# Attention on one core: a planner's list of steps replaced by a finished order

## The chip, the cores and the metric

The kernel runs on one core of a Trainium2 chip. The metric is device time in microseconds of one launch; lower is better. TensorE (PE in the profile) does matmuls, ScalarE (ACT) and VectorE (DVE) elementwise work, GpSimd (POOL) the same and DMA issues, SyncE (SP) DMA issues alone. Each engine takes its instructions strictly in the order in which the program lists them.

## The reference

Grouped-query attention: 8 batches, 8 query heads, 2 key/value heads, 1024 positions, head size 64, all float32.

```python
for g in range(n_kv_heads):
    q_group = q[:, g*4:(g+1)*4]; k_group = k[:, g:g+1]; v_group = v[:, g:g+1]
    scores = np.matmul(q_group, k_group.transpose(0, 1, 3, 2)) / np.sqrt(64)
    attn = np.exp(scores - scores.max(-1, keepdims=True))
    output[:, g*4:(g+1)*4] = np.matmul(attn / (attn.sum(-1, keepdims=True) + 1e-08), v_group)
```

The kernel leaves the maximum out, which changes nothing at this size of scores, and divides after the second matmul.

## The kernel before, in words

There are 64 jobs, one for each batch and head, numbered b * 8 + h. A job is cut into 8 tiles along the keys. A tile is 128 keys by 1024 queries of scores: two concurrent matmuls of 64 rows (line 761, a "pair") write it to one of three slots of PSUM, `sp0` to `sp2`, of two banks each. A tile is then turned into exponentials in one of two ways.

- On ScalarE: one activation (line 771) from the slot to a bfloat16 tile `pt`. 368 of the 512 tiles go this way.
- On VectorE: 144 tiles. A first pass (line 783, `p` in the list below) scales the scores and writes 16-bit integers `yt`, which frees the slot. A chain of one or two such tiles then gets three steps out of SBUF: the mantissa part `zt` (line 792, "zh"), the exponent part `et` (line 800, "two"), and the product of `yt` and `zt` (line 810, "mul"). The exponential is the sum of `et` and `zt`; the output matmuls add it by reading both tiles, and in the last three jobs VectorE adds it itself (line 816). Columns of the product are given to GpSimd in pieces (line 739). VectorE and GpSimd do not use the shared port at the same time: a piece is tied to run beside the passes out of PSUM.

The output matmuls (line 829) take a 128 x 128 block of exponentials as weights and 65 columns of `va`, which are the 64 columns of v and a column of ones for the sum. Eight pieces of 128 queries make a job; seven pieces fill a bank (`ops`), then VectorE takes reciprocals of the sums (line 894) and multiplies (line 904) into `ost`, and SyncE stores a job of 256 KB (line 913). Jobs 0 and 63 are done tile by tile (lines 849 and 869).

Inputs come in by DMA. GpSimd's queue casts q, k and v from float32 to bfloat16 in DRAM (line 519; from job 4 on two jobs of q at a time). SyncE's queue transposes q (line 588) and k (line 578) into SBUF and copies the two halves of the transposed k to each other's partitions (lines 582 and 583), so that tiles 4 to 7 can be read as well, and loads v (line 571). A DMA on SyncE whose input has not landed holds up those behind it.

What sets the order: `Plan` walks through a string `ORDER` of steps and gives each step a model time from constants (the `M_` lines). The events are sorted by that time and emitted. `W` in the string means that PE's model waits; a score is only placed when its slot is free in the model. When casts, transposes and copies go out is worked out from the model time at which a job's first score is due (`need`): the transposes of q 11 us ahead of it, of k 12.5, the copies 6.5.

Of the kernel before, what the change touches and what calls it, by code (L numbers as in the profile page):

```python
# [108 lines left out]


class Chain:


    def __init__(self, id, nsteps):
        self.id, self.nsteps = id, nsteps
        self.pairs = []
# [4 lines left out]
        self.zend = INF
        self.end = 0

class State:
    pass


class Plan:

    def __init__(self, nj, npt, nct, nyt):
        self.nj, self.npt, self.nct, self.nyt = nj, npt, nct, nyt

# [3 lines left out]
        self.groups += [(i, min(i + PB, self.last)) for i in range(NPIECE, self.last, PB)]  # L140
# [807 lines left out]
```

## Time and profile before

| what | value |
| --- | --- |
| median of three runs | 353.0 us (352.84 to 353.11) |
| span of the profiled execution, first to last instruction | 350.8 us |
| own time of the profiled execution | not listed apart from its span; the median is 2.2 us above the span |
| PE busy (matmuls, ends modelled) | 342.2 us |
| ACT busy | 342.3 us |
| DVE busy | 340.5 us |
| POOL busy | 276.9 us |

Busy time is the union of an engine's instructions. Instructions that overlap in their pipelines make an engine look busy though the next one started late, so for ACT and DVE the distance between starts says more than the busy share. A row of the timeline is start, length, engine, line, operation, output<-input, shape and count of merged instructions; in brackets the idle time ahead of it and what ended it. A row of the groups is count, busy time, mean of one in ns, idle time ahead of them and what ended it. In a row by windows each engine's busy time is followed by the number of its instructions in brackets, then come the granted clock of PE, the share of the DMA engines and GB/s.

### The profile page before, as it was taken

The page shows a single profiled execution, that of the slowest core. Times are in us where ns is not written, and L with a number is a line of the kernel's source. Part 1 is how long each engine was busy: PE and PEld are TensorE (multiplying, and loading weights), DVE is VectorE, ACT ScalarE, POOL GpSimd, SP SyncE. Part 2 cuts the span into 40 slices and gives each one's busy share as a digit, 9 for nine tenths or more (in the row PEclk, how much of TensorE's full clock was granted, in tenths as well). Part 3 has the DMA queues.
Part 4 walks back from the last instruction along what each step waited for, and adds up shares of the span by engine and source line. Part 5 has one row for each costly group of instructions (what it writes and reads, how often), then busy time and mean ns, then how long its engine had stood idle before and what let it go on. Part 6 is the DMA issues. An engine that isn't in the chain of part 4 may idle for free.

```text
span 350.8 us, 14254 instructions
## 1 busy us (share of the span) xinstructions
PE 342.2 (98%) x6272; PEld 224.9 (64%) x6272; DVE 340.5 (97%) x517; ACT 342.3 (98%) x372; POOL 276.9 (79%) x265
## 2 busy tenths in 40 slices
PE   7899999999999999999999999999999999999995
PEld 3466666666666666666666666666666676666674
DVE  5999999999999999999999999999999999999995
ACT  6999999999999999999999999999999999999994
POOL 3268889799999999898999998999989958982000
PEclk9999999999999999999999999999999999999999
DMA  6899766496749757769896977297767994453223
GB/s 150 121 165 167 140 120 146 84 151 139 136 92 137 148 124 134 129 132 124 125 157 120 151 138 122 64 191 135 122 127 107 170 168 119 107 122 74 69 76 109
DMA packets 96574, 44.84 MB, mean 128 GB/s; under 512 B 61168, under 2 KB 95344, under 8 KB 95728
## 3 DMA queue, kind: packets, MB, share of 16 engines
q1 hardware_dynamic: 94128, 31.34, 43.8%
q0 software_dynamic: 2096, 12.19, 26.5%
q8 instruction: 49, 0.80, 1.1%
q10 hardware_dynamic: 288, 0.39, 0.3%
q14 instruction: 13, 0.11, 0.1%
HBM read 27.13 MB, written 28.97 MB: 160 GB/s over the span
## 4 chain that ended last, share of the span: by engine, by line
PE 60%; ACT 21%; DVE 15%; issue 1%; DMA 1%; DVEq 0%
PE ops L829 32%; PE sp L761 27%; ACT pt L771 21%; DVE yt L783 8%; DVE et L800 2%; DVE ost L904 2%; DVE zt L792 1%; DVE zt L810 1%; DMA q<-in_q_dram 1%; PE sp L869 1%; DVE rec L894 1%; PE sp L644 0%; DVE qt L662 0%; ACT q L633 0%; DVEq L943 0%
## 5 line engine op out<-in xcount | busy, mean ns | idle before, releaser
L771 ACT ACTIVATE pt<-sp 128x1024 bf16<-128x1024 f32 x368 | 339.8, 1036 | 0.5 <-PE sp L761 0.3
L739 POOL TENSOR_TENSOR zt<-yt,zt 128x560 bf16<-128x560 bf16 (+15 forms) x151 | 238.3, 1583 | 28.3 <-DVE zt L792 10.1
L829 PE MATMUL ops<-va,pt 128*128 128x65 bf16 x2840 | 177.0, 194 | 0.0
L783 DVE TENSOR_SCALAR yt<-sp 128x1024 uint16<-128x1024 f32 x144 | 174.9, 1215 | 1.3 <-PE sp L761 1.2
L761 PE MATMUL sp<-qt,kt 64*128 64x512 bf16 x1024 | 168.9, 382 | 3.2 <-ACT pt L771 1.7
L829 PEld LDWEIGHTS <-pt 128*128 128x128 bf16 x2840 | 131.5, 97 | 32.8 <-issue 32.8
L829 PE MATMUL ops<-va,zt 128*128 128x65 bf16 x1128 | 131.1, 194 | 0.0
L829 PE MATMUL ops<-va,et 128*128 128x65 bf16 x1096 | 125.3, 194 | 0.0
L829 PEld LDWEIGHTS <-et 128*128 128x128 bf16 x1096 | 87.9, 98 | 15.2 <-issue 15.0
L829 PEld LDWEIGHTS <-zt 128*128 128x128 bf16 x1128 | 91.2, 97 | 9.6 <-issue 9.2
L761 PEld LDWEIGHTS <-kt 64*128 64x128 bf16 x1024 | 50.9, 93 | 59.0 <-issue 36.0
L792 DVE TENSOR_SCALAR zt<-yt 128x2048 uint16<-128x2048 uint16 (+1 forms) x73 | 49.8, 683 | 0.5
L800 DVE TENSOR_SCALAR et<-yt 128x2048 uint16<-128x2048 uint16 (+1 forms) x73 | 49.0, 675 | 0.0
L904 DVE TENSOR_TENSOR ost<-ops,rec 128x448 f32<-128x448 f32 (+2 forms) x73 | 44.7, 612 | 0.5
L810 DVE TENSOR_TENSOR zt<-yt,zt 128x928 bf16<-128x928 bf16 (+17 forms) x64 | 39.1, 611 | 0.0
L519 POOL DMA_DIRECT2D qd<-in_q_dram x33 | 21.6, 655 | 4.4 <-PE sp L761 3.6
L894 DVE RECIPROCAL rec<-ops 128x7 f32<-128x7 f32 (+2 forms) x73 | 14.5, 199 | 0.1
L734 POOL MEMSET tick<- 128x1 bf16 x57 | 12.0, 211 | 0.0
L519 POOL DMA_DIRECT2D kd<-in_k_dram x8 | 5.3, 657 | 5.1 <-PE sp L761 5.1
L621 PE MATMUL ops<-warm 128*128 128x128 bf16 (+1 forms) x24 | 4.6, 334 | 1.2 <-DVE warm L513 1.2
L519 POOL DMA_DIRECT2D vd<-in_v_dram x8 | 5.6, 700 | 0.0
L621 PEld LDWEIGHTS <-warm 128*128 128x128 bf16 x24 | 2.0, 114 | 3.5 <-issue 2.3
(39 smaller groups left out, 27.4 us busy)
## 6 DMA issues: line engine op xcount, KB each, us to landing
out_dram<-ost SPq DMA_DIRECT2D x63, 256.0 KB, 3.1
qd<-in_q_dram POOLq DMA_DIRECT2D x29, 256.0 KB, 5.0
kt<-kt SPq DMA_DIRECT2D x30, 64.0 KB, 3.4
va<-vd SPq DMA_DIRECT2D x30, 64.0 KB, 3.1
kd<-in_k_dram POOLq DMA_DIRECT2D x7, 256.0 KB, 4.5
vd<-in_v_dram POOLq DMA_DIRECT2D x7, 256.0 KB, 5.3
qt<-qd SPq DMA_TRANSPOSE x63, 4.5
qd<-in_q_dram POOLq DMA_DIRECT2D x5, 128.0 KB, 4.0
```

Of the source, the lines that this page charges most:

```text
L519: return nc.gpsimd.dma_start(out=t.rearrange("(a x) d -> a (x d)", a=128), in_=src.rearrange("(a x) d -> a (x d)", a=128),)
L734: early = nc.gpsimd.memset(tick, 0.0)
L739: begun[j] = gps = nc.gpsimd.tensor_tensor(out=z, in0=flat(yt[j])[:, lo : lo + w], in1=z, op=ALU.mult)
L761: now = nc.tensor.matmul(sps[x][:, half, :], lhsT=t[lo : lo + D, c // NH, ci % NH * 128 : (ci % NH + 1) * 128], rhs=qt[j][lo : lo + D, 0, ...
L771: exps.append(nc.scalar.activation(out=p, in_=where_s[(j, c)], func=AF.Exp, scale=scale))
L783: vec = nc.vector.tensor_scalar(out=yt[ch][:, i, :, :], in0=where_s[c], scalar1=EXP_A, scalar2=EXP_B, op0=ALU.mult, op1=ALU.add,)
L792: vec = nc.vector.tensor_scalar(out=zt[j][:, 0:c], in0=yt[j][:, 0:c], scalar1=0x7F, scalar2=0x3F00, op0=ALU.bitwise_and, op1=ALU.bitwise_or,)
L800: vec = ins = nc.vector.tensor_scalar(out=et[j][:, 0:c], in0=yt[j][:, 0:c], scalar1=0x7F80, scalar2=None, op0=ALU.bitwise_and,)
L810: vec = nc.vector.tensor_tensor(out=z, in0=flat(yt[j])[:, 0 : cols[0]], in1=z, op=ALU.mult)
L829: ended[job] = nc.tensor.matmul(ops[plan.group_of[x] % 2][:, lo : lo + D + 1], lhsT=p[:, qs * 128 : (qs + 1) * 128], rhs=va[(b * G + h // ...
L894: vec = nc.vector.reciprocal(out=to, in_=sums)
L904: vec = nc.vector.tensor_tensor(out=to, in0=src, in1=by, op=ALU.mult)
```

## The change

The planner goes: the model constants, `State`, `Plan` and its sorting by time are removed. `ORDER` is now the finished list of instructions for all engines, in which every step stands as it is to be emitted, DMAs among them, with the slot that a score uses and the columns that GpSimd takes. New letters: `A0` a ScalarE score into slot 0, `a1` to `g1` a score for VectorE of the job 0 to 6 ahead into slot 1, `x` the activation, `p` VectorE's first pass, `z`, `t`, `m`, `+` the steps of the chain so many chains back, `G1,197` a piece of 8 x 197 columns of the chain one back, `V` three output matmuls, `r` and `n` reciprocal and normalisation, `S` a store, `X`, `q`, `Y`, `k`, `Z`, `v` casts, `T`, `K` transposes, `C` the two copies of k, `U` loads of v. `W` is gone: a score stands where it stands, and PE waits there if the slot is not free.

- A VectorE tile is now mostly three or four jobs ahead of ScalarE's (124 of 144 tiles); before, mostly one (82), at most two.
- `yt`, `et` and `zt`, pools of 6, 8 and 8 chains, become two rings of 22 tiles, `ye` and `zz`. The exponent step works in place on `ye`, so it now stands behind the product and waits for GpSimd's piece, which reads `ye`.
- GpSimd's pieces change from 151 to 111; 34 of them have 1392 to 1592 columns, where the longest was 928. The columns that are left to VectorE fall from 57,912 to 46,176 over all chains. Chains of one tile: 2 before, 8 now; of two: 71 before, 68 now. The last three jobs have 8 VectorE tiles instead of 5.
- The ring of transposed q has 12 buffers instead of 8; q is cast earlier.
- The exponent step waits for the store four stores back; before, for those older than 10 us in the model.
- PE's dummy matmuls fall from 24 to 14.

```diff
-PB = 7 ... M_NORM = 531          (some 35 constants of the model)
+NPT = 34
+NYT = 22
+NQT = 12
 ORDER = """
-AaApFFFFWWWWFFAWWWWWWWWWWWWWWWWWWWWaWWWWWWWWWWApEEWWEA0bWWWApEFFWWWAW0WWWaEpAEWWA0WWAWWWWWWAFFF0FE0E
...
+A0IX3TY1a1xA2TpxA0za1KxA2pE0E2xFA0m0E3xb1zA2t1E5X4FxpFA0E1xX6m0A2b1zE6xpA0E7FxFA2t1Cb1zxA0pG0,63E4xT
+A2rzc1xG1,65nA0pxA2G0,15Tm2A1xZ1b0G0,25rY2nt2xG0,70A2pSVTVVVVxVX8VVVzA1c0xm1A2pG0,65TVVVVVVxVVVt1A1b
...
 """
-class Plan: ...
-    qp = ctx.enter_context(tc.tile_pool(name="qp", bufs=8))
-    yp = ctx.enter_context(tc.tile_pool(name="yp", bufs=NYT))
-    ep = ctx.enter_context(tc.tile_pool(name="ep", bufs=NCT))
-    zp = ctx.enter_context(tc.tile_pool(name="zp", bufs=NCT))
+    qp = ctx.enter_context(tc.tile_pool(name="qp", bufs=NQT))
+    ye = kvp.tile([128, NYT, 2, HS], U16, name="ye")
+    zz = kvp.tile([128, NYT, 2, HS], U16, name="zz")
...
-    for when, kind, x, j, c, *cols in ev:
+    for kind, arg in re.findall(r"([A-Za-z+])([0-9,]*)", "".join(ORDER.split())):
...
+        elif kind == "C":
+            copy_k(*cp_next.pop(0))
...
+        elif kind == "T":
+            turn_q(tq_next)
+            tq_next += 1
...
+        elif kind == "G":
+            ch = chains[-1 - arg[0]]
+            w = 8 * arg[1]
+            ch.cols -= w
...
+            z = flat(ch.tiles(zz))[:, ch.cols : ch.cols + w]
+            gps = nc.gpsimd.tensor_tensor(
+                out=z, in0=flat(ch.tiles(ye))[:, ch.cols : ch.cols + w], in1=z, op=ALU.mult
+            )
+            tc.add_manual_dep(gps.ins, gate.ins.name, Sync, reason="the port goes to the step behind it")
...
-            et[j] = ep.tile([128, CHN, 2, HS], U16, name="et")
-            vec = ins = nc.vector.tensor_scalar(
-                out=et[j][:, 0:c], in0=yt[j][:, 0:c], scalar1=0x7F80, scalar2=None,
+            vec = nc.vector.tensor_scalar(
+                out=ch.tiles(ye), in0=ch.tiles(ye), scalar1=0x7F80, scalar2=None,
                 op0=ALU.bitwise_and,
             )
-            while stores and stores[0][0] < when - 10000:
+            while len(stores) > 3:
...
```

SyncE's queue in the first 25 us. `qt` of `qd3` is job 3's transposed q, of `qd4` jobs 4's and 5's; `kt` of `kd0_1` is the k of batch 0, group 1, which jobs 4 to 7 read. Before:

```order
L588 DMA_TRANSPOSE qt_224<-qd3_178 128x1x512
L578 DMA_TRANSPOSE kt_283<-kd0_1_182 128x1x512
L588 DMA_TRANSPOSE qt_312<-qd4_267 128x1x512
L588 DMA_TRANSPOSE qt_383<-qd4_267 128x1x512
L582 DMA kt_283<-kt_283 64x512
L583 DMA kt_283<-kt_283 64x512
L913 DMA out_0_dram<-ost_101 128x512
```

And now:

```order
L243 DMA_TRANSPOSE qt_185<-qd3_171 128x1x512
L233 DMA_TRANSPOSE kt_197<-kd0_1_175 128x1x512
L237 DMA kt_197<-kt_197 64x512
L238 DMA kt_197<-kt_197 64x512
L243 DMA_TRANSPOSE qt_355<-qd4_256 128x1x512
L243 DMA_TRANSPOSE qt_380<-qd4_256 128x1x512
L378 DMA out_0_dram<-ost_92 128x512
```

The two copies of k's halves have moved from behind the transposes of jobs 4 and 5 to ahead of them.

PE's list at the first scores of job 4 (the pair that reads `qt_312` before, `qt_355` now; `qt_224` is job 3, `qt_173` job 2). Before, the pair stands in the output matmuls that follow the scores of ScalarE's 21st tile:

```order
L829 LDWEIGHTS pt_307
L829 MATMUL ops1_522<-va0_102,pt_307 128x65
L761 LDWEIGHTS kt_283
L761 MATMUL sp2_544<-qt_312,kt_283 128x512
L761 LDWEIGHTS kt_283
L761 MATMUL sp2_544<-qt_312,kt_283 128x512
L829 LDWEIGHTS et_486
L829 MATMUL ops1_522<-va0_102,et_486 128x65
```

And now:

```order
L400 MATMUL sp1_443<-qt_173,kt_111 128x512
L400 LDWEIGHTS kt_111
L400 MATMUL sp1_443<-qt_173,kt_111 128x512
L400 LDWEIGHTS kt_197
L400 MATMUL sp0_446<-qt_355,kt_197 128x512
L400 LDWEIGHTS kt_197
L400 MATMUL sp0_446<-qt_355,kt_197 128x512
L400 LDWEIGHTS kt_111
L400 MATMUL sp2_452<-qt_173,kt_111 128x512
L400 LDWEIGHTS kt_111
L400 MATMUL sp2_452<-qt_173,kt_111 128x512
```

It has moved up, between the scores of ScalarE's 17th tile (`sp1_443`) and of its 18th (`sp2_452`).

VectorE in the middle of the program. Before, the steps of the chains lie in changing places between the passes out of PSUM (L783) and the normalisations:

```order
L800 TENSOR_SCALAR et<-yt 128x2048
L783 TENSOR_SCALAR yt<-sp_4613 128x1024
L894 RECIPROCAL rec<-ops_4530 128x7
L810 TENSOR_TENSOR zt<-yt,zt 128x80
L904 TENSOR_TENSOR ost<-ops_4530,rec 128x448
L792 TENSOR_SCALAR zt<-yt 128x2048
L800 TENSOR_SCALAR et<-yt 128x2048
L783 TENSOR_SCALAR yt<-sp_4710 128x1024
L810 TENSOR_TENSOR zt<-yt,zt 128x1248
```

And now:

```order
L560 RECIPROCAL rec<-ops_4220 128x7
L422 TENSOR_SCALAR ye<-sp_4362 128x1024
L571 TENSOR_TENSOR ost<-ops_4220,rec 128x448
L422 TENSOR_SCALAR ye<-sp_4402 128x1024
L457 TENSOR_TENSOR zz<-ye,zz 128x472
L431 TENSOR_SCALAR zz<-ye 128x2048
L463 TENSOR_SCALAR ye<-ye 128x2048
L560 RECIPROCAL rec<-ops_4356 128x7
L422 TENSOR_SCALAR ye<-sp_4474 128x1024
```

Two passes and a normalisation now stand together, with the three steps of a chain behind them, and GpSimd's long piece of 1392 to 1592 columns lies beside the first four.

More of the change, by code (lines that the diff above doesn't have):

```diff
@@ new lines, with __init__, tiles @@
+VnA1A0m2xVSVVVVVVVVVVxVVrVt2A2A1nxVVVVVVzVSVVVxVVzA0m1A2VxVVVVVVrVVt1xVVVA1nA0xV+1VVSVVVVVVxVVVVVm0A
+2b1xrA0pVVVVVVxVVVVt0A2A1zxVVnVVVVVVm0VVVSxA0A2rt0VVnVxVVVVVV+1VVSVVxVVV+0VL0,1L1,1L4,1rnL5,1L6,1L2,
+1SL3,1L7,1rn
+"""
+LENGTHS = """
+1111122122222222222222222222222222222222222222222222222222222222222222222211
+"""
+class Chain:
+    def __init__(self, at, n):
+        self.at, first = at, at % NYT
+        self.first, self.n = first, n
+        self.cols = 1024 * n
+        self.parts = 0
+    def tiles(self, ring):
+        return ring[:, self.first : self.first + self.n]
@@ L438, with groups_of @@
+def groups_of(nj):
+    last = (nj - 1) * NPIECE
+    groups = [(0, NPIECE // 2), (NPIECE // 2, NPIECE)]
+    groups += [(i, min(i + PB, last)) for i in range(NPIECE, last, PB)]
+    return groups + [(last, last + NPIECE)]
 @with_exitstack
@@ new lines, in half @@
+    def half(j, par, ci):
+        return [p[:, par] for _, p in terms(j, par, [ci])]
+    for kind, arg in re.findall(r"([A-Za-z+])([0-9,]*)", "".join(ORDER.split())):
+        arg = [int(x) for x in arg.split(",")] if arg else []
+        if kind == "X":
+            begin("q", arg[0], True)
+        elif kind == "Y":
+            begin("k", divmod(arg[0], G), True)
+        elif kind == "Z":
+            begin("v", divmod(arg[0], G), True)
+        elif kind == "q":
+            begin("q", arg[0], False)
+        elif kind in "kv":
+            begin(kind, (arg[0], 0), False)
+        elif kind == "K":
+            turn_k(*kt_next.pop(0))
+        elif kind == "C":
+            copy_k(*cp_next.pop(0))
+        elif kind == "U":
+            fill_v(*fv_next.pop(0))
+        elif kind == "I":
+            place_v(0, 0)
+        elif kind == "T":
+            turn_q(tq_next)
+            tq_next += 1
+        elif kind == "S":
+            r = place_of(st_next * NPIECE)
+            ins = nc.sync.dma_start(
+                out=rows(out[divmod(st_next, H)], st_next == 0),
+                in_=ost[:, r : r + NPIECE, :].rearrange("p (s two) d -> p s (two d)", two=2),
+            )
+            stores.append(ins)
+            st_next += 1
+        elif kind in "Aabcdefg":
+            while nxt[a] == NC:
+                a += 1
+            j, x = a + (0 if kind == "A" else "abcdefg".index(kind)), arg[0]
+            c = nxt[j]
+            nxt[j] += 1
@@ L909 @@
                         )
-        elif kind == "store":
-            b, h = divmod(j, H)
-            r = place_of(j * NPIECE)
-            ins = nc.sync.dma_start(
-                out=rows(out[b, h], j == 0),
-                in_=ost[:, r : r + NPIECE, :].rearrange("p (s two) d -> p s (two d)", two=2),
-            )
-            stores.append((when, ins))
 _INS = ['q', 'k', 'v']
```

694 lines of the change are left out of this document (164 added, 530 removed).

## The prediction

> **What bounds the kernel now.** I read the page first, then the timeline of ScalarE, because the page says that three engines are full at once.
>
> ```profile
> span 350.8 us, 14254 instructions
> PE 342.2 (98%) x6272; PEld 224.9 (64%) x6272; DVE 340.5 (97%) x517; ACT 342.3 (98%) x372; POOL 276.9 (79%) x265
> ...
> L771 ACT ACTIVATE pt<-sp 128x1024 bf16<-128x1024 f32 x368 | 339.8, 1036 | 0.5 <-PE sp L761 0.3
> ```
>
> The exponentials of line 771 have only 0.5 us of idle time before them, so ScalarE looks like a hard bound. Its timeline shows that this is not quite so: one lasts 1036 ns, but the starts lie 924 apart, and a start that comes late by less than that overlap leaves no idle gap.
>
> ```profile
> 6.05 339.90 ACT L771 ACTIVATE pt<-sp 128x1024 bf16<-128x1024 f32 x368 [0.34 <-PE sp L761]
> ...
> 331.03 9.28 ACT L771 ACTIVATE pt<-sp 128x1024 bf16<-128x1024 f32 x10
> 340.11 1.11 ACT L771 ACTIVATE pt<-sp 128x1024 bf16<-128x1024 f32 x1
> ...
> 45.70 3.06 ACT L771 ACTIVATE pt<-sp 128x1024 bf16<-128x1024 f32 x3
> 47.74 1.94 ACT L771 ACTIVATE pt<-sp 128x1024 bf16<-128x1024 f32 x2
> ```
>
> The first row is the whole stream: 368 tiles in 339.9 us, 0.924 each. Ten tiles start between 331.03 and 340.11, so 0.908 each is possible. If every tile went at that pace the stream would be 368 x (0.924 - 0.908) = 5.9 us shorter; that is the most that any order of the same 368 tiles can take out of the middle. The last two rows are a place where it is lost: two tiles take 47.74 - 45.70 = 2.04 us, 0.22 more than at the good pace. TensorE shows why.
>
> ```profile
> 46.38 0.20 PE L829 MATMUL ops<-va,zt 128*128 128x65 bf16 x1
> ...
> 47.31 0.39 PE L761 MATMUL sp<-qt,kt 64*128 64x512 bf16 x2
> ```
>
> The score pair at 47.31 ends at 47.70 and the tile starts at 47.74: it waited for its scores, and those stood behind 0.93 us of output matmuls. So in this kernel a late tile is a score that PE reached late, while PE itself is not the bound in total.
>
> **The change in the steady part.** The counts of tiles do not change: 368 exponentials on ScalarE and 144 tiles on VectorE before and now. What is freed is VectorE's multiply, which moves to GpSimd (57,912 columns before, 46,176 now, from the order lists).
>
> ```profile
> L792 DVE TENSOR_SCALAR zt<-yt 128x2048 uint16<-128x2048 uint16 x71 | 49.0, 690 | 0.5
> L800 DVE TENSOR_SCALAR et<-yt 128x2048 uint16<-128x2048 uint16 x71 | 48.2, 682 | 0.0
> L810 DVE TENSOR_TENSOR zt<-yt,zt 128x2048 bf16<-128x2048 bf16 x8 | 9.7, 1209 | 0.0
> L810 DVE TENSOR_TENSOR zt<-yt,zt 128x640 bf16<-128x640 bf16 x8 | 3.8, 476 | 0.0
> ...
> L816 DVE TENSOR_TENSOR zt<-et,zt 128x2048 bf16<-128x2048 bf16 x2 | 2.5, 1225 | 0.1
> L792 DVE TENSOR_SCALAR zt<-yt 128x1024 uint16<-128x1024 uint16 x2 | 0.8, 423 | 0.0
> L800 DVE TENSOR_SCALAR et<-yt 128x1024 uint16<-128x1024 uint16 x2 | 0.8, 419 | 0.0
> L816 DVE TENSOR_TENSOR zt<-et,zt 128x1024 bf16<-128x1024 bf16 x1 | 0.7, 694 | 0.0
> ```
>
> The two multiply rows give (1209 - 476) / 1408 = 0.52 ns a column, so 11,736 columns less are -6.1 us. Chains of one tile grow from 2 to 8 and chains of two fall from 71 to 68: the mantissa step (line 792) costs 6 x 423 - 3 x 690 = +0.5 us, the exponent step (line 800) 6 x 419 - 3 x 682 = +0.5. The last three heads have 8 VectorE tiles where they had 5, so the final add (line 816) goes from 2 x 1225 + 694 to 3 x 1225 + 2 x 694, +1.9 us. In sum VectorE has 3.2 us less to do. TensorE has 34 matmuls less, 10 of them dummies; at the 0.93 us that the 27 above took that is 1.2 us. Stretches of more than 27 output matmuls in a row fall from 25 to 13 in the order lists. GpSimd gets 11,736 columns more in 111 pieces instead of 151:
>
> ```profile
> L739 POOL TENSOR_TENSOR zt<-yt,zt 128x560 bf16<-128x560 bf16 x69 | 109.4, 1586 | 9.8 <-DVE et L800 2.2 <-DVE yt L783 1.8 <-DVE zt L792 1.4
> L739 POOL TENSOR_TENSOR zt<-yt,zt 128x848 bf16<-128x848 bf16 x21 | 44.8, 2133 | 5.1 <-DVE rec L894 3.2 <-DVE et L800 1.3 <-DVE zt L810 0.5
> ```
>
> That is (2133 - 1586) / 288 = 1.90 ns a column and 0.52 us a piece: +22.3 - 20.9 = +1.4 us on an engine that is busy for 276.9 of 350.8, hidden.
>
> Two waits are new on VectorE, and all of its work is queued behind them. The exponent step now overwrites the tile that GpSimd's piece reads, so it waits for that piece; ahead of it stand a multiply and a mantissa step, 0.48 and 0.69 us in the rows above, so a piece may be about a microsecond late before it costs anything. It also waits for the store of the fourth head back, which is some 20 us old where a store lands in 3 (the row is in the DMA fence below). Both 0. The deeper rings of q and of y and z remove limits that the waits of this profile do not show: 0.
>
> What this is worth on ScalarE has no row; it lies between two ends. The upper end is the whole 5.9 us, which would need every late score gone. The lower end is a loss of 1 us, if scores that now wait in place hold up output matmuls behind them. Thirteen long stretches instead of 25 would leave 13/25 of the lateness if it came from them alone, a gain of 5.9 x 12/25 = 2.8; but lateness also comes from a score that waits for VectorE, and those waits stay. I take 2.0 us, between nothing and that share, and nearer the share since VectorE too has 3.2 us more slack.
>
> **The change in the first 25 us.** Here SyncE's queue has another order, shown with the change. The two copies of k's halves (L582 and L583, now L237 and L238) have moved ahead of the transposes of head 4's q (qt of qd4). They read the transposed k of L578 (now L233), so SyncE cannot issue them until it has landed, and everything behind them on that queue waits too: head 4's and 5's q, the first store, head 6's q.
>
> ```profile
> 10.95 1.26 SPq L578 DMA_TRANSPOSE kt<-kd  x1
> 16.32 2.61 SPq L588 DMA_TRANSPOSE qt<-qd  x2
> 19.04 0.55 SPq L582 DMA_DIRECT2D kt<-kt  x1
> 19.63 0.59 SPq L583 DMA_DIRECT2D kt<-kt  x1
> 20.31 0.54 SPq L913 DMA_DIRECT2D out_dram<-ost  x1
> ```
>
> ```profile
> kt<-kd SPq DMA_TRANSPOSE x1, 7.3
> ...
> qt<-qd SPq DMA_TRANSPOSE x1, 5.1
> ...
> qt<-qd SPq DMA_TRANSPOSE x2, 6.2
> ...
> out_dram<-ost SPq DMA_DIRECT2D x63, 256.0 KB, 3.1
> ...
> kt<-kd SPq DMA_TRANSPOSE x15, 5.8
> ...
> qt<-qd SPq DMA_TRANSPOSE x63, 4.5
> ...
> qt<-qd SPq DMA_TRANSPOSE x1, 2.5
> ```
>
> The second fence is the DMA view, time from issue to landing: the k transpose issued at 10.95 (7.3 us), head 4's q issued at 16.32 (5.1), that q and the next together (6.2), the medians of all stores, k and q transposes, and the fastest, the first q. What stands ahead of the k transpose does not move: its own issue behind the casts and head 3's q stays at 10.95. So k lands at 18.25, the copies go out at 18.3 and 18.9, and head 4's q at about 19.4 instead of 16.32. At 5.1 us, the row of that very transfer, it lands at 24.5. The earlier q casts do not help, as that cast is not what it now waits for.
>
> Meanwhile PE needs it sooner. The first scores of head 4 have moved on PE from behind the scores of ScalarE's 21st tile to between those of its 17th (sp1_443) and its 18th (sp2_452). PE takes its list in order, so the 18th tile's scores wait for head 4's q.
>
> ```profile
> 6.05 14.81 ACT L771 ACTIVATE pt<-sp 128x1024 bf16<-128x1024 f32 x16 [0.34 <-PE sp L761]
> ...
> 23.82 0.39 PE L761 MATMUL sp<-qt,kt 64*128 64x512 bf16 x2
> ...
> 45.84 0.61 PE L761 MATMUL sp<-qt,kt 64*128 64x512 bf16 x4 [0.18 <-DVE yt L783]
> ```
>
> Before, head 4's first score starts at 23.82, behind its landing at 16.32 + 5.1 = 21.4, and waits for nothing. Now the 17th tile starts at 6.05 + 16 x 0.92 = 20.7 and ends its share at 21.6. The q lands at 24.5, two score pairs take 0.61, and the 18th tile starts at 25.1: ScalarE stands for 3.5 us, and as it is the fullest engine nothing gives that back. The ends: with the fastest q transpose (2.5) it lands at 21.9 and the wait is 0.9; with the 6.2 of the pair 25.6 and 4.6. With both medians (5.8 and 4.5) k lands at 16.8, q goes at 17.9 and lands at 22.4, a wait of 1.4. I take 3.5, because the rows are those of the same transfers at the same place beside the same casts. Zero is not excluded, if the other DMAs fall differently.
>
> The parts before the first score and after the last exponential are the same work in the same order; 0, give or take 0.3 us.
>
> **Sum.** 350.8 + 3.5 - 2.0 = 352.3 us for the span. The page gives the profiled execution no other time than this span; the median of the runs is 353.0, so 2.2 us lie around it, and I predict 354.5 us. A measurement of this kernel can tell about 0.2% (0.7 us) from no change.
>
> **Rivals.** First, the other side: the wait at head 4 is short. It decides below 2.0 us, that is when head 4's q lands before 23.0, 3.6 us after its issue or with k landed earlier than 16.8. With no wait at all the time is 353.0 - 2.0 = 351.0; with the medians it is 353.0 + 1.4 - 2.0 = 352.4. The 2.5 us row speaks for it, the 5.1 and 6.2 of this very place against. Second, PE's clock: an idle PE may be slowed.
>
> ```profile
> 346.00:346.80 0.80, 0.79 (x24) 0.62 (x19) 0.14 (x1) 0.00 (x0) 0.00 (x0) 1.00 0.05 15
> 346.80:349.40 2.60, 0.00 (x0) 0.00 (x0) 0.82 (x3) 0.00 (x0) 0.00 (x0) 1.00 0.65 197
> 349.40:350.70 1.30, 0.00 (x0) 0.00 (x0) 0.00 (x0) 0.00 (x0) 0.00 (x0) 0.51 0.00 0
> 14.90:18.30 3.40, 2.19 (x25) 0.88 (x21) 3.37 (x7) 3.40 (x5) 0.86 (x2) 1.00 0.48 83
> ```
>
> In these rows the value behind POOL's is the granted clock: it falls to 0.51 after PE has been idle for 2.6 us, at the end, and stays at 1.00 in the thinnest stretch with work. A wait of 3.5 us is longer than 2.6. If it needs the same 2.6 us of work to come back, half a clock costs at most 1.3 us: 355.8. The Trainium skill, "TensorE: Matmul & The Clock Gate", Part 1, says that one idle window of about 3.4 us halves the clock and that the windows run freely, not from the kernel's start. By it the drop would come in some executions and not in others, and half a window lost would be 1.7 us, 356.2. The trace agrees on the drop, and shows nothing on its phase. Third, no gain in the steady part: GpSimd's new pieces of 1576 columns take 0.52 + 1576 x 1.90 = 3.5 us, and if VectorE's next locked step has to wait for them, lateness stays as it is and only the early wait is left: 356.5. The 560 and 848 rows fit their cover now, and nothing shows one of that length.
>
> **Chances.** Early wait of 2.4 us or more with the gain and no slow clock (forecast, 353.2 to 355.7): 0.37. The same with the slow clock, 0.18. Early wait without the gain, 0.08. Short wait, faster: 0.28. Wait and gain that cancel to within 0.7 us: 0.09 outside the forecast's own range. That makes faster 0.29, same 0.13 and slower 0.58, a little of the forecast's lower edge counted as the same. The range reaches from no wait (351.0) to no gain (356.5), 350.8 to 356.6.
>
> **What would show it.** In the new profile PE should have one idle stretch that starts near 21 us, released by the DMA of qt, with a gap of about 3.5 us before ScalarE's 18th tile, and the copies at L237 should be issued no sooner than 18 us. A granted clock under 1.00 near 25 us is the second rival. The 350 tiles behind it should run at under 0.92 us each; at 0.924 the third rival holds. If the copies go out near 15 us the prediction is wrong and the kernel is faster.

## The result, and the profile after

The changed kernel takes 358.6 us (median of 4 runs, 358.1 to 360.0), the kernel before 353.1 on the same chip (352.8 to 353.4): a ratio of 1.0169, 95% interval 1.0153 to 1.0185. The forecast was 354.5 with a range up to 356.6. The direction and the place were right; the time lies 2.0 us above the range. The profiled execution took 359.0 us itself, 1.8 more than its span, where the forecast put 2.2.

The page of the changed kernel, first the span, the engines and ScalarE's row, then the clock in fortieths of the span:

```profile
span 357.2 us, 14129 instructions
PE 343.3 (96%) x6238; PEld 225.2 (63%) x6238; DVE 341.1 (95%) x524; ACT 340.8 (95%) x372; POOL 289.5 (81%) x221
...
PEclk9987999999999999999999999999999999999998
...
L411 ACT ACTIVATE pt<-sp 128x1024 bf16<-128x1024 f32 x368 | 338.2, 1080 | 7.2 <-PE sp L400 7.2
```

ScalarE now has 7.2 us of idle time before its tiles instead of 0.5, all of it for scores, and the clock has a dip in the third and fourth slices. SyncE's timeline shows the queue:

```profile
10.82 1.26 SPq L233 DMA_TRANSPOSE kt<-kd  x1
18.01 0.54 SPq L237 DMA_DIRECT2D kt<-kt  x1
18.59 0.59 SPq L238 DMA_DIRECT2D kt<-kt  x1
19.27 2.54 SPq L243 DMA_TRANSPOSE qt<-qd  x2
```

The copies go out at 18.01, and head 4's q behind them at 19.27 (16.32 before). PE's timeline and its clock by windows (the value behind POOL's):

```profile
26.12 1.04 PE L400 MATMUL sp<-qt,kt 64*128 64x512 bf16 x4 [5.02 <-DMA qt<-qd]
...
21.00:24.00 3.00, 0.10 (x2) 0.00 (x0) 1.60 (x2) 1.16 (x2) 2.73 (x3) 1.00 1.00 154
24.00:27.00 3.00, 0.88 (x4) 0.16 (x4) 0.23 (x1) 0.00 (x0) 0.00 (x0) 0.50 1.18 160
27.20:31.00 3.80, 3.80 (x49) 2.35 (x49) 2.68 (x4) 2.29 (x3) 1.97 (x2) 0.52 1.92 166
31.00:60.00 29.00, 28.84 (x516) 18.58 (x513) 28.67 (x44) 29.00 (x32) 26.42 (x17) 1.00 0.70 136
```

PE stands for 5.02 us until the q has landed at 26.0, 6.7 us behind its issue, and from 24.0 us to 30.8 it has half its clock. ScalarE's timeline, with the last store that it issues; behind the "..." the same store of the kernel before:

```profile
6.46 15.70 ACT L411 ACTIVATE pt<-sp 128x1024 bf16<-128x1024 f32 x17 [0.62 <-PE sp L400]
27.19 1.02 ACT L411 ACTIVATE pt<-sp 128x1024 bf16<-128x1024 f32 x1 [5.03 <-PE sp L400]
29.33 1.02 ACT L411 ACTIVATE pt<-sp 128x1024 bf16<-128x1024 f32 x1 [1.12 <-PE sp L400]
30.75 320.45 ACT L411 ACTIVATE pt<-sp 128x1024 bf16<-128x1024 f32 x349 [0.39 <-PE sp L400]
353.67 0.35 ACTq L573 DMA_DIRECT2D out_dram<-ost  x1
...
347.69 0.35 ACTq L906 DMA_DIRECT2D out_dram<-ost  x1
```

These rows account for the 6.4 us between the spans (350.8 and 357.2); 0.918 and 0.9235 us are the mean distances of the starts, now (349 tiles) and before (all 368):

| where | worked out | us | forecast |
| --- | --- | --- | --- |
| first tile | 6.46 - 6.05 | +0.4 | 0 ± 0.3 with the tail |
| wait for head 4's q | idle ahead of the 18th tile | +5.0 | +3.5 |
| 18th to 20th tile | 30.75 - 27.19 - 2 x 0.923 | +1.7 | a rival, +1.3 |
| 348 starts behind it | 348 x (0.918 - 0.9235) | -1.9 | -2.0 |
| last tile's end to end of span | 6.0 (357.2 - 351.2) against 4.85 | +1.2 | 0 ± 0.3 with the start |

### The profile page after: what moved, and what is told of

Its sections match the earlier page's. It is cut to its first block, busy times and chain, and to the rows that moved or that the text cites. A ratio compares the mean times of both kernels' runs of the same rounds, so it can differ in the third digit from the quotient of the medians.

```text
span 357.2 us, 14129 instructions
## 1 busy us (share of the span) xinstructions
PE 343.3 (96%) x6238; PEld 225.2 (63%) x6238; DVE 341.1 (95%) x524; ACT 340.8 (95%) x372; POOL 289.5 (81%) x221
## 4 chain that ended last, share of the span: by engine, by line
PE 48%; ACT 42%; DMA 6%; issue 1%; SPq 1%; DVE 0%; POOL 0%; DVEq 0%
ACT pt L411 42%; PE ops L491 26%; PE sp L400 22%; DMA kt<-kd 2%; DMA qt<-qd 2%; DMA vs<-in_v_dram 1%; DMA qd<-in_q_dram 1%; PE sp L529 1%; SPq L243 0%; SPq L253 0%; SPq L238 0%; SPq L237 0%; POOL va L210 0%; DVE ost L571 0%; DVEq L602 0%
## 5 line engine op out<-in xcount | busy, mean ns | idle before, releaser
L448 POOL TENSOR_TENSOR zz<-ye,zz 128x624 bf16<-128x624 bf16 (+28 forms) x111 | 246.2, 2218 | 32.7 <-DVE zz L431 15.5
L422 DVE TENSOR_SCALAR ye<-sp 128x1024 uint16<-128x1024 f32 x144 | 175.8, 1221 | 6.8 <-PE sp L400 5.5
L491 PE MATMUL ops<-va,pt 128*128 128x65 bf16 x2864 | 162.7, 195 | 0.0
L491 PE MATMUL ops<-va,zz 128*128 128x65 bf16 x1104 | 121.7, 194 | 0.0
L491 PE MATMUL ops<-va,ye 128*128 128x65 bf16 x1072 | 117.9, 194 | 0.0
L491 PEld LDWEIGHTS <-ye 128*128 128x128 bf16 x1072 | 81.9, 98 | 15.2 <-issue 14.6
L491 PEld LDWEIGHTS <-zz 128*128 128x128 bf16 x1104 | 84.4, 98 | 7.7 <-issue 7.7
L431 DVE TENSOR_SCALAR zz<-ye 128x2048 uint16<-128x2048 uint16 (+1 forms) x76 | 50.5, 670 | 0.1
L463 DVE TENSOR_SCALAR ye<-ye 128x2048 uint16<-128x2048 uint16 (+1 forms) x76 | 49.5, 659 | 0.0
L457 DVE TENSOR_TENSOR zz<-ye,zz 128x2048 bf16<-128x2048 bf16 (+25 forms) x63 | 33.0, 525 | 0.0
```

Source lines behind the costliest of these rows:

```text
L422: vec = nc.vector.tensor_scalar(out=ye[:, i, :, :], in0=where_s[(j, c)], scalar1=EXP_A, scalar2=EXP_B, op0=ALU.mult, op1=ALU.add,)
L431: vec = nc.vector.tensor_scalar(out=ch.tiles(zz), in0=ch.tiles(ye), scalar1=0x7F, scalar2=0x3F00, op0=ALU.bitwise_and, op1=ALU.bitwise_or,)
L448: gps = nc.gpsimd.tensor_tensor(out=z, in0=flat(ch.tiles(ye))[:, ch.cols : ch.cols + w], in1=z, op=ALU.mult)
L457: vec = nc.vector.tensor_tensor(out=z, in0=flat(ch.tiles(ye))[:, 0 : ch.cols], in1=z, op=ALU.mult)
L463: vec = nc.vector.tensor_scalar(out=ch.tiles(ye), in0=ch.tiles(ye), scalar1=0x7F80, scalar2=None, op0=ALU.bitwise_and,)
L491: ended[job] = nc.tensor.matmul(ops[g % 2][:, lo : lo + D + 1], lhsT=p[:, par, qs * 128 : (qs + 1) * 128], rhs=va[(b * G + h // HPG) % NVA ...
```

## The experiments

Letters of `ORDER` as in the section on the change; only the piece that changes is shown.

**The copies behind the q again.**

```diff
-A2t1Cb1z ... G0,15Tm2
+A2t1b1z  ... G0,15TCm2
```

> The changed kernel, with one thing put back: SyncE's two copies of k's halves (L237, L238) stand behind the transposes of head 4's and head 5's q again, the rest of the order as changed. Theory (the copies hold up the queue): head 4's q is issued near 16 us instead of 19.27, lands near 21 to 22, PE's idle stretch before the 18th tile falls from 5.0 to under 1.5 us, the granted clock stays at 1.00, and the time is 351 to 352.5 us, 6 to 7 under the changed kernel. Rival (the q comes late for another reason, its cast or the transfer itself): the q still lands after 24 us and the time stays over 356.

352.84 us (351.97 to 354.75), ratio to before 1.0006, 0.9992 to 1.0021. So 5.8 us go with the place of two DMAs (5.4 when each of the two kernels is set against the kernel before as timed beside it). SyncE's timeline, PE's wait, and the windows:

```profile
14.62 2.81 SPq L243 DMA_TRANSPOSE qt<-qd  x2
17.52 0.55 SPq L237 DMA_DIRECT2D kt<-kt  x1
...
PE sp L400 <- DMA qt<-qd: 1.1, 1, 1.1
...
15.00:18.00 3.00, 1.57 (x22) 0.80 (x19) 1.96 (x5) 2.64 (x4) 2.22 (x3) 1.00 0.59 120
18.00:21.00 3.00, 2.44 (x24) 1.33 (x24) 2.97 (x6) 3.00 (x4) 1.52 (x3) 0.58 0.40 106
```

The queue theory holds and its rival falls. The time is 0.3 us above what was expected, and one part missed: the clock fell (to 0.50 from 18.5 to 21.9; 0.58 is the mean of the second row) although PE stood for 1.1 us at the longest, behind a stretch in which it was busy for 1.57 of 3 us.

**The same queue order in the kernel before.**

```diff
-            ev.append((at - 6500, "cp", None, (b, g), None))
+            ev.append((at - (11500 if j == 4 else 6500), "cp", None, (b, g), None))
```

> The kernel before, with one thing changed: SyncE's two copies of that k's halves (L582, L583) stand ahead of the transposes of head 4's q, as in the changed kernel; PE's order is that of before, where head 4's first score came at 23.8 us. Theory (the queue alone makes the q late, the earlier use on PE makes the wait longer): the q lands near 26 us, PE stands for about 2.3 us, perhaps too short for the clock to drop, and the time is 355 to 356 us, 2 to 3 over before. Rival (the queue order costs nothing without the earlier use): 353.0, no change.

354.55 us (352.60 to 356.34), ratio 1.0061, 1.0025 to 1.0098. PE's and ScalarE's timelines:

```profile
25.61 0.39 PE L761 MATMUL sp<-qt,kt 64*128 64x512 bf16 x2 [1.91 <-DMA qt<-qd]
...
27.08 320.77 ACT L771 ACTIVATE pt<-sp 128x1024 bf16<-128x1024 f32 x347 [1.83 <-PE sp L761]
```

The queue alone costs 1.9 us, just under what was expected, and a wait of 1.91. Of the other 3.1 us of the changed kernel's wait, 2.6 are the earlier use on PE, which stops at 21.1 there and at 23.7 here, and 0.5 the later landing. The two runs with a clock of 1.00 took 354.1 and 354.6, two with 0.995 and 0.994 took 356.1 and 356.3: some 1.9 us apart, as a fall of the clock would have it. That cause is not shown, since only the run of 354.6 has a trace; the fifth, 352.6 with a clock of 0.997, fits neither pair and stays open.

**PE kept busy in the wait.** `F` is a dummy matmul that no result uses.

```diff
-VVVzA1c0xm1A2p
+VVVzA1F...F(80 times)c0xm1A2p
```

> The changed kernel, with 80 dummy matmuls that no result uses put on TensorE between the 17th tile and the wait for head 4's q, so that PE is not idle while it waits (some 4 us of work; the q still lands near 26 us). Theory (the wait and the slow clock are two separate costs): the granted clock stays at 1.00 up to 31 us, tiles 18 to 20 start 0.92 apart, and the time falls by the 1.7 us that those three tiles lost, to 357 us. Rival (those tiles came late for their scores' order, not for the clock): tiles 18 to 20 stay late and the time stays at 358.6; a second rival, the dummies themselves delay the scores: above 358.6.

357.04 us (356.86 to 357.24), ratio 1.0128, 1.0111 to 1.0145. The DMA view of head 4's q alone, PE's timeline, windows and ScalarE's timeline:

```profile
qt<-qd SPq DMA_TRANSPOSE x1, 3.9
...
22.02 4.64 PE L269 MATMUL ops<-warm 128*128 128x128 bf16 x80
...
18.00:21.00 3.00, 2.37 (x23) 1.26 (x23) 2.96 (x6) 3.00 (x4) 1.44 (x3) 0.53 0.48 101
24.00:27.00 3.00, 3.00 (x52) 2.60 (x49) 0.00 (x0) 0.00 (x0) 0.37 (x1) 1.00 0.95 205
...
27.24 1.02 ACT L411 ACTIVATE pt<-sp 128x1024 bf16<-128x1024 f32 x1 [4.09 <-PE sp L400]
28.50 321.31 ACT L411 ACTIVATE pt<-sp 128x1024 bf16<-128x1024 f32 x350 [0.23 <-PE sp L400]
```

The 18th tile starts where it did (27.24 and 27.19), but not because of the q. In this execution the q, issued at 18.75, had landed at 22.7, not near 26, and the dummies themselves held its scores until 26.6. So what the two traces compare is a delay of the same end, with PE idle in one and busy in the other. The clock had fallen here too, to 0.50 from 18.2 to 21.6, in the thin part ahead of the dummies, which was not expected; behind the delay it is at 1.00. The 20th tile then starts 2.2 us behind the 18th (at 29.42) instead of 3.6, 0.3 more than two good tiles take. The time is 1.6 us less than the changed kernel's, 1.2 when each is set against the kernel before as timed beside it. The delay and the slow clock behind it are two costs that add.

**Why the q took so long to land.**

```diff
-A1xZ1b0G0,25rY2nt2xG0,70A2pSVTVVVVxVX8VVVzA1c0xm1A2pG0,65T
+A1xb0G0,25rnt2xG0,70A2pSVTVVVVxVVVVzA1c0xm1A2pG0,65Z1Y2X8T
```

> The changed kernel, with the three GpSimd casts that are issued at 18.8 to 21.8 us (v of the second group, k of the next, q of heads 8 and 9; 128 to 256 KB each) moved behind GpSimd's piece of 520 columns, so that they go out after head 4's q transpose has landed. The copies still stand ahead of that q. Theory (the q took 6.8 us instead of the 5.1 of before because those casts ran beside it): it is issued near 19.3 as now, lands 4 to 5 us later, the wait of PE falls from 5.0 to about 3, and the time to 356 to 357 us. Rival (the casts are not what slows it): the q takes 6.8 us again and the time stays at 358.6.

356.97 us (355.63 to 357.45), ratio 1.0118, 1.0102 to 1.0134. The DMA view of the issues from 19 to 21 us, changed kernel first, then this one (median time to landing last), and PE's wait here:

```profile
kd<-in_k_dram POOLq DMA_DIRECT2D x1, 256.0 KB, 5.7
vd<-in_v_dram POOLq DMA_DIRECT2D x1, 128.0 KB, 3.3
...
qt<-qd SPq DMA_TRANSPOSE x2, 6.6
```

```profile
qt<-qd SPq DMA_TRANSPOSE x2, 2.6
...
22.34 0.61 PE L400 MATMUL sp<-qt,kt 64*128 64x512 bf16 x4 [1.68 <-DMA qt<-qd]
```

With no cast issued beside them the transposes land in 2.6 us instead of 6.6, more than expected. The other traces agree for head 4's q alone: 2.4 to 2.8 us in the six in which no cast was issued within 2.5 us on either side of it (this kernel, the first one, and four below), 4.1 with a cast 2.2 us ahead of it (the kernel with the k cast moved last), 3.9 with the first cast 0.8 us behind it (the kernel with PE kept busy), 5.1 with it 0.7 behind (the kernel before), 6.3 and 6.7 with casts issued less than 1 us ahead of it (the kernel before with the copies ahead, and the changed kernel). Less than the 3.3 us of wait came back in the time, 1.7, because the casts now make GpSimd late elsewhere: the 24th tile waits 1.43 us for its scores (the trace is of the fastest run, 355.6; the other three took 356.6 to 357.5). VectorE's and GpSimd's timelines:

```profile
25.83 2.97 DVE L431 TENSOR_SCALAR zz<-ye 128x2048 uint16<-128x2048 uint16 x1
...
26.80 1.44 POOL L448 TENSOR_TENSOR zz<-ye,zz 128x656 bf16<-128x656 bf16 x1
```

The mantissa step takes 2.97 instead of 0.69 us and ends 0.56 us after GpSimd's piece. The Trainium skill, "SBUF — State Buffer", "Who interferes with whom", says that VectorE in its fast modes and GpSimd lock a shared pair of ports against each other for a whole instruction; the rows agree.

**What is left with the copies put back.** The next kernels start from that one. First, head 4's q cast earlier:

```diff
-A2TpxA0za1Kx ... E5X4Fxp
+A2TX4pxA0za1Kx ... E5Fxp
```

> The kernel with the copies put back behind head 4's and 5's q, and in addition the cast of head 4's q (on GpSimd) moved forward, to where the second q transpose is issued. Theory (with the copies out of the way the q lands near the moment of need, so an earlier cast takes away what is left): no idle stretch of PE before the 18th tile, time 0 to 1 us under the kernel with the copies alone put back, 350.5 to 351.5. Rival (the cast holds up other casts and transposes ahead of the first heads): the start of the stream or an early tile is late by up to 1 us, no gain or a loss of up to 1 us.

352.68 us (352.05 to 353.20), ratio 0.9998, 0.9989 to 1.0008: the wait for q falls to 0.3 us, the time does not come out under before. The rows show one reason, a mantissa step that waits for a late piece of GpSimd and a 20th tile that is 0.85 us late behind it: VectorE's and GpSimd's timelines, then ScalarE's.

```profile
20.33 1.59 DVE L431 TENSOR_SCALAR zz<-ye 128x2048 uint16<-128x2048 uint16 x1
...
20.11 1.25 POOL L448 TENSOR_TENSOR zz<-ye,zz 128x560 bf16<-128x560 bf16 x1
...
24.30 320.44 ACT L411 ACTIVATE pt<-sp 128x1024 bf16<-128x1024 f32 x349 [0.85 <-PE sp L400]
```

So I moved the two casts that make that piece late:

```diff
-A1xZ1b0G0,25rY2nt2xG0,70A2pS ... G0,65T
+A1xb0G0,25rnt2xG0,70Z1A2pS ... G0,65Y2T
```

> The kernel with the copies put back and the earlier cast, with two more casts moved on GpSimd: v of the second group behind the piece of 560 columns instead of ahead of that of 200, k of the next heads behind the piece of 520 instead of ahead of that of 560. Theory (the casts make GpSimd's pieces late, the 560 one then runs beside VectorE's mantissa step at 20.3 us, which takes 1.59 instead of 0.69 us, holds up a score bank and costs ScalarE 0.85 us at its 20th tile): the step takes 0.7 again, PE's wait for VectorE of 1.0 us is gone, and the time falls by 0.9 to 351.8 us, under both kernels. Rival (something else is late there as well, or later casts make v or k late): 352.7 or more.

353.46 us (352.48 to 356.16), ratio 1.0043, 1.0021 to 1.0064, in two groups: seven runs at 352.5 to 353.6 and five at 355.5 to 356.2. The step is on time and the 1.0 us wait of PE gone, and still the kernel is slower. VectorE's timeline and the window:

```profile
20.52 0.69 DVE L431 TENSOR_SCALAR zz<-ye 128x2048 uint16<-128x2048 uint16 x1
...
20.00:22.00 2.00, 2.00 (x29) 1.40 (x27) 1.32 (x3) 1.34 (x3) 1.98 (x4) 0.50 0.75 221
```

The clock is at 0.50 there, behind 4 us in which PE was busy for 2.63, and all twelve runs have a mean clock of 0.993 to 0.995. That a stretch is thin is not enough: in the changed kernel PE was busy for 2.65 us from 16 to 20, and the clock stayed at 1.00. I filled the thin stretch ahead of it:

```diff
-E4xTA2rzc1xG1,65nA0pxA2G0,15TCm2A1xb0G0,25rnt2xG0,70Z1A2pS
+E4(4 F)xTA2rzc1(4 F)xG1,65nA0(8 F)pxA2(6 F)G0,15TCm2A1(6 F)xb0(4 F)G0,25rnt2xG0,70Z1A2(4 F)pS
-            dummy(1, 128, 1 - group_of[pc] % 2, beside=0 < fleft < NC)
+            dummy(1, 128, 1 - group_of[pc] % 2, beside=fleft < NC)
```

> The last kernel (copies put back, earlier cast, two casts later), with 32 dummy matmuls that no result uses in the stretch from 16 to 20 us, where TensorE has only score pairs to do (2.6 of 4 us busy). There the granted clock fell to 0.50 from 20.0 to 22.8 us, which cost tiles 16 to 20 about 1.7 us. Theory (the thin stretch lowers the clock, and the lower clock makes these tiles late): the clock stays at 1.00, the first 20 tiles start 0.92 apart, the time falls by 1.5 to 1.8 us to about 351.8, under both kernels, and the spread of its runs (352.5 to 356.2) shrinks. Rival (the dummies stand ahead of the scores and delay them, or the clock falls anyway): 353 or more.

355.86 us (354.73 to 356.92), ratio 1.0079, 1.0058 to 1.0100, with 36 dummies, not 32: a new wait in place of the old. The waits of VectorE up to 31 us:

```profile
DVE rec L560 <- PE ops L269: 1.6, 1, 1.6
```

The dummies write the bank that VectorE's second division reads, so it waits for them, GpSimd's pieces come late, and the step at 26 us takes 2.83 us. With 28 dummies in the other bank, all behind the division that reads that one:

```diff
-E4(4 F)xTA2rzc1(4 F)xG1,65nA0
+E4xTA2rzc1xG1,65nA0
-            dummy(1, 128, 1 - group_of[pc] % 2, beside=fleft < NC)
+            dummy(1, 128, 1 - group_of[pc] % 2 if fleft else 0, beside=fleft < NC)
```

> The dummies of the run before in the other output bank, 28 of them, all behind the division that reads that bank, so that VectorE's second division has no dummies to wait for (in the run before it waited 1.55 us for them, and GpSimd's late pieces then ran beside the mantissa step at 26 us, 2.83 instead of 0.69 us). Theory (thin stretch lowers the clock, lower clock costs tiles 16 to 20 some 1.7 us): clock 1.00, no wait of VectorE, time 1.5 us under the same kernel without dummies (353.46), about 351.8, where the piece of 624 columns ends before the mantissa step. Rival (GpSimd's lateness decides, not the clock): clock 1.00 and yet 353 or more, with a mantissa step of over 1.5 us beside a GpSimd piece.

351.70 us (351.39 to 352.59), ratio 0.9967, 0.9954 to 0.9980: the one whole computation here that beats both kernels, 1.2 us under before. All five runs have a mean clock of 0.999 or 1.000, and the window is at full clock (in the trace, which is of the slowest run, PE waits 1.1 us for the q):

```profile
20.00:22.00 2.00, 1.94 (x39) 1.42 (x37) 1.94 (x3) 1.86 (x3) 2.00 (x2) 1.00 0.63 195
```

Last, the cast of k moved on again, with its transpose:

```diff
-G0,65Y2T ... rzb0v1xKVVpA2G1,82VVV
+G0,65T ... rzb0v1xVVpA2G1,82Y2KVVV
```

> The same, with the cast of the next heads' k moved again, from ahead of the piece of 624 columns to behind that of 656, and its transpose on SyncE with it. In the kernel without dummies the 624 piece ended 0.36 us ahead of the mantissa step in the profiled execution, and its other runs fell into two groups, near 353 and near 355.6. Theory (the second group is the collision of that piece with the mantissa step, and the cast of 0.55 to 0.8 us ahead of it decides which): all runs in one group, 351.0 to 352, under both kernels. Rival (the two groups come from something else, as the landing of head 4's q): two groups again, over 2 us apart.

355.20 us (354.50 to 356.81), ratio 1.0071, 1.0054 to 1.0089. Neither theory: SyncE's timeline and PE's waits show the first fault of this change once more.

```profile
24.80 1.41 SPq L226 DMA_DIRECT2D va<-vd  x2
32.57 1.72 SPq L233 DMA_TRANSPOSE kt<-kd  x1
34.39 4.77 SPq L243 DMA_TRANSPOSE qt<-qd  x2
...
PE sp L400 <- DMA qt<-qd: 2.4, 2, 1.5
```

The k transpose waits for the later cast until 32.57, the transposes of the next q stand behind it, and PE waits 2.4 us for them. What made the two groups of runs without dummies stays open: all of those runs had nearly the same mean clock. With the 28 dummies there was one group. With the 36 there were two again, and these go with the clock: three runs at 354.7 to 355.1 with 1.000, three at 356.7 to 356.9 with 0.993 to 0.995, some 1.8 us apart.

**The steady part and the tail.** Two kernels from that with the earlier cast, with output matmuls left out by

```diff
+                if i == 1 and 64 <= pc < 448 and pc % 6 < 1:
+                    continue
```

and by the same with `pc % 3 < 2`.

> The kernel with the copies put back and the earlier cast, with 64 output matmuls left out, one in every sixth row piece between heads 8 and 55 (its second term; those output sums lack it). Theory (TensorE is the bound of the steady part: it has no waits there, and the tiles come when its row of matmuls lets them): 64 x 0.0305 = 1.95 us less, all of it seen in the stream of tiles, 25th to last from 315.75 to 313.8 us, and in the time: 350.7 us. Rival (ScalarE or VectorE is the bound and PE fills its gaps): the stream stays at 315.75 and the time at 352.7.

> The same with 256 output matmuls left out (two of three row pieces between heads 8 and 55 lack their second term). On TensorE alone this would be 7.8 us. Theory: the stream follows until ScalarE's own pace of 0.908 us a tile (ten tiles in a row showed it before) is reached, which is 3.3 us under now, and the output matmuls behind the last tile fall back to before's: 348.5 to 349 us, with idle time of PE <- ACT for the first time. Rival (VectorE, 99% busy there too, stops it sooner): 350 to 351 us, with PE waiting for VectorE.

352.22 us (ratio 0.9985, 0.9976 to 0.9995) and 352.76 (1.0003, 0.9992 to 1.0015). My theory falls: 256 matmuls less give nothing. ScalarE's timeline, and the chain that ended last by line, with 256 less; behind the first "..." the chain of the kernel they start from, behind the second a pair of scores on PE and two tiles of ScalarE, again with 256 less:

```profile
24.46 320.23 ACT L411 ACTIVATE pt<-sp 128x1024 bf16<-128x1024 f32 x349 [0.85 <-PE sp L400]
by line: ACT pt L411 85.2%; PE ops L493 2.9%; DVE ye L422 2.7%; PE sp L400 2.4%; issue 1.1%; DVE zz L431 1.0%; DMA q<-in_q_dram 0.9%; PE sp L531 0.6%; DVE zz L457 0.6%; DVE ye L463 0.3%; DVE ost L573 0.2%; PE sp L292 0.2%; DVE kt L313 0.2%;
...
by line: ACT pt L411 43.0%; PE ops L491 25.9%; PE sp L400 21.9%; DMA qt<-qd 1.6%; DMA vs<-in_v_dram 1.3%; DVE ye L422 1.0%; DMA qd<-in_q_dram 1.0%; issue 0.9%; PE sp L529 0.6%; DVE zz L431 0.5%; DVE ost L571 0.2%; SPq L253 0.2%; DVE zz L457
...
78.21 0.39 PE L400 MATMUL sp<-qt,kt 64*128 64x512 bf16 x2
77.64 1.16 ACT L411 ACTIVATE pt<-sp 128x1024 bf16<-128x1024 f32 x1
78.64 1.07 ACT L411 ACTIVATE pt<-sp 128x1024 bf16<-128x1024 f32 x1
```

349 tiles take 320.23 us instead of 320.44, and the chain, with hardly any of PE left in it, runs along ScalarE. That does not show ScalarE's own pace. As the prediction says of the kernel before, a tile that is late by less than the overlap leaves no idle gap, and the last rows are such a tile: its scores end at 78.60, it starts at 78.64, 1.00 us behind the one ahead. Counted over the tiles behind the 25th, those that start within 0.06 us of the end of a pair of scores are 117 of 343 before (on average 0.942 us behind the tile ahead; the others 0.914), 90 in the changed kernel (0.933; 0.912) and 80 with 256 matmuls less (0.938; 0.911). So the gain of the steady part is fewer late scores, as the prediction argued: tiles 25 to 368 start within 314.7 us in the changed kernel and 316.8 before. And with 256 matmuls less there are still 80 late tiles, worth some 2 us by these means (80 x 0.027, an estimate). What holds their scores stays open; the others come 0.911 apart, near the 0.908 of the ten good tiles.

For the tail, the same with `480 <= pc < 504`, 24 matmuls:

> The kernel with the copies put back and the earlier cast, with 24 output matmuls left out in heads 60 to 62 (one a row piece; those sums lack a term). TensorE's last output matmul ended 1.41 us behind the end of the last exponential, against 0.84 before, although 256 matmuls less up to head 55 changed nothing. Theory (the last three heads' output matmuls are what TensorE is late with): 24 x 0.0305 = 0.7 us less, and PE ends 0.7 us behind the last exponential; the time falls by 0.7, to 352.0. Rival (the end is set by the order, the last matmuls waiting for the last tile or for VectorE's last adds): 1.4 us as before, no change in the time.

351.88 us (ratio 0.9968, 0.9956 to 0.9980), 0.8 under the kernel with all of them, about what was expected. ScalarE's and PE's timelines:

```profile
25.07 320.44 ACT L411 ACTIVATE pt<-sp 128x1024 bf16<-128x1024 f32 x349 [0.85 <-PE sp L400]
...
346.15 0.41 PE L531 MATMUL sp<-va,pt 128*128 128x65 bf16 x8
```

PE ends at 346.56, 1.05 us behind the last tile's end at 345.51, where it was 1.41. So the backlog of PE in the last three heads is real, but only 0.36 us of it is gone by this, and the rest of the 0.8 is not accounted for. The backlog is there in every trace of the changed order that keeps these matmuls: PE ends 1.39 to 1.42 us behind the last tile, against 0.84 before. The other part of the tail lies behind PE's end: from the last store's issue to the end of the span it took 2.7 us here, 3.1 before, 3.5 in the changed kernel, in other traces of the changed order 2.7 to 3.8. That is a spread between executions, and its cause stays open.

## Why the prediction was right and wrong

- **The queue: right.** Copies expected at 18.3, seen at 18.01; the q at 19.4, seen at 19.27. The first two kernels above show both halves, queue and earlier use.
- **The size of the wait: wrong, the first failed step.** "At 5.1 us, the row of that very transfer, it lands at 24.5": it took 6.7 and landed at 26.0. The row was of the same transfer, but not beside the same casts: before, the first cast went out 0.7 us behind it (at 17.0, the transfer at 16.32). Issued 3 us later, it had a cast of 128 KB 0.5 us ahead of it, one of 256 KB 0.8 us behind and another at 2.6. With no cast near it, it lands in 2.4 to 2.8. I had taken the end of 4.6 us as the outer bound; 5.0 lies beyond it.
- **The slow clock: wrong, the second.** It was a rival with 0.18, priced at 1.3 us from its own row, while the row that was quoted said that the clock falls after 2.6 us idle and the forecast was a wait of 3.5. It belonged in the sum as a consequence of the wait. It lasted 6.8 us and cost up to 1.7; PE kept busy gave 1.2 to 1.6 back. By the Trainium skill, "TensorE: Matmul & The Clock Gate", Part 1, the drop comes with an idle window of 3.4 us that runs freely, so in some executions only; in the changed kernel all four showed a mean clock of 0.982 to 0.987, and the first experiment shows a fall with no idle stretch over 1.1 us.
- **The steady part: right.** -1.9 against -2.0, and by the mechanism named, fewer late scores (90 tiles instead of 117). The size was a choice between two ends, so that it came out so close is in part luck. That the whole 5.9 us could be had is not shown: some 2 us of late scores are left with 256 matmuls less.
- **Start and tail: wrong, the third.** "The same work in the same order; 0, give or take 0.3 us": the order of the last heads is another, and PE ends 0.56 us later behind the last tile; the last store goes out 0.17 us later still, and the other 0.5 of the +1.2 lies in the part that spreads between executions. The +0.4 at the start is most likely spread too: the kernels above whose lists are the same up to the first tile start it at 5.82 to 6.63.
- **No gain in the steady part, the third rival: did not happen** there, but its mechanism, a GpSimd piece that holds VectorE, did, at 20 us, where late casts pushed it.

Together: +1.5, +1.7, +0.4 and +1.2 are 4.8 of the 4.9 us between the forecast span (352.3) and the profiled one (357.2). The times are 4.1 apart (354.5 and 358.6), because a run takes 1.8 us more than its span and not 2.2, and the profiled execution lies 0.4 above the median.

## What to carry to other kernels

In a queue that is served in order, look for what each DMA waits for itself: one that cannot start holds up all behind it, and two rows in another place cost more than twice the gain of a re-ordered steady part. A wait of PE as long as those after which the clock fell here (2.6 us in the prediction's row, 2.9 into the wait of the changed kernel) is to be priced with the slow clock behind it, and a transfer that moves in time is to be priced with the transfers that it then runs beside. A cast that moves in GpSimd's list moves the pieces behind it: pieces late by about 1 us made a step of VectorE 0.9 to 2.3 us longer. And a chain that runs along the fullest engine does not show that the engine has no late starts; count how many start just behind their inputs.

## What the runs showed of the hardware

- Two q transposes landed in 2.6 us with no cast issued beside them, and in 6.6 beside three casts of 640 KB in all; one alone in 2.4 to 2.8 with none near, in six traces.
- The granted clock fell to 0.50 for 3.4 us behind stretches in which PE was 52% to 66% busy (1.57 of 3.00 us; 2.63 of 4.00), with no idle stretch over 1.1 us; 28 dummies kept it at 1.00, and with them the time was 1.8 us less. In other traces it stayed at 1.00 behind stretches as thin (2.65 of 4.00 us in the changed kernel; 1.93 of 3.40 in that with the later casts), so they give no threshold.
- A mantissa step of 0.69 us took 1.59 to 2.97 beside a GpSimd multiply, and ended 0.55 to 0.57 us after that multiply in five traces.
